# Modulation sums spread past the output projection, and a 32-byte tile in the last pool

## The chip, the cores and the metric

The kernel runs on one core of a Trainium2 chip. The metric is device time of one execution in microseconds (us), the median of several runs. Before the change it is 2329.75 us, the median of three (2326.13 to 2329.98).

## The reference, cut to what matters

One encoder layer for a sequence of 512 rows of width 2048, in fp32:

```
mod = silu(c) @ w_ada + b_ada                     # six vectors of 2048: sh1, sc1, gt1, sh2, sc2, gt2
h   = rms_norm(x, g_norm1) * (1 + sc1) + sh1
proj = h @ w_in                                   # q, k, v of 8 differential heads; latents of 8 MLA heads
a_out = subln(softmax(q1 k1 + bias) - lam * softmax(q2 k2 + bias)) @ v
b_out = latent attention with rotary tails
x   = x + gt1 * (concat(a_out, b_out) @ w_out)    # the output projection, residual x1
h2  = rms_norm(x, g_norm2) * (1 + sc2) + sh2      # needs all of x1's row, sh2 and sc2
x   = x + gt2 * ((silu(h2 @ w_gate) * (h2 @ w_up)) @ w_down)
```

## The kernel before

**Three matmuls for one.** Every fp32 product is computed from split operands: hi is the value rounded to TensorE's fp32r format, lo the remainder, and `mm3` (L240 to L243) issues hi*hi, lo*hi and hi*lo. Weights are split on the way: a chunk of 128x1024 is loaded into one of 3 `raw` buffers (L73), ScalarE casts hi (L89), and VectorE or GpSimd subtracts to get lo (L97). Which of the two does it stands in the plan: "dve", "pool", or "alt" for taking turns. There are two buffers for lo in these stages, so a split waits until TensorE is done with the chunk two before, and a load until the chunk three before is split.

**Stages.** Input projection and both attentions run to about 780 us. Then the output projection goes over four column blocks of 512 (L1072): blocks 0, 2 and 3 have 96 matmuls left, block 1 has 192, in chunks of 24; behind each block stand its residual (L1053 multiplies by `gt1`, L1054 adds to `x1`), a store of `x1` to DRAM (`x1d`, read back at the very end), and the squares' sums on ScalarE (L1102). The transposes of a block's `x1` (L1060) stand 36 matmuls into the next block. After block 3 come its transposes, the reciprocal root `rstd2` (a reduction on VectorE, two steps on GpSimd, L260 and L261) and its broadcast by matmul (`ps_r`). Then two gate/up column blocks in plain form (`gate_up`, 384 matmuls each), whose operand `h2` is built on the way by `second_norm` (L1134 to L1136) and `combine`; then the other gate/up blocks in a Strassen-like form to about 1818 us, and the down projection (`ps_d`, 2112 matmuls), which reads activations back from DRAM into `ax` tiles.

**The second modulation.** `mod2` (L1069) is a generator for columns 1024 to 2047 of sc2 and sh2. For each of two groups of 4 column chunks it loads 32 pieces of `w_ada` (256 KB each, L301) into `x1` slots, of which there are 24 (X_SLOTS), shared with `x1`, its transposes and the sums; VectorE multiplies each by a column of silu(c) and adds it to `adaacc` (L305, L308: the sums, 64 in all); then `ada_columns` turns the two sums of a group into columns by eight matmuls against a vector of ones (`ps_ada`, L327; each is recorded twice). That makes 78 steps, and `MOD_PACE` says how many are taken at each of the 8 or 16 yields (12 matmuls) of a block; `second_norm` takes what is missing for its group.

**Order.** TensorE's order is the order of the calls. The other engines' queues, and the loads on SP's queue, are put in order by the language's scheduler from its own estimates, so a number in `MOD_PACE` moves instructions on all of them. Each engine runs its queue in order: an instruction that waits holds all behind it.

**Places in SBUF.** The last pool, `fd` (L1351), is filled from the right-hand end: `sums`, `gt2`, then the `ax` tiles and `x1r`. In the built program the `ax` tiles begin at byte 126,944 of each partition, 32 beyond a multiple of 64, in steps of 2,048; the split weights of the down stage begin at 44,480 and on in steps of 4,096, multiples of 64. `ax` is the stationary operand of the down matmuls, the weights the moving one. In the output projection and gate/up both operands lie 32 beyond a multiple of 64; in the scores of the differential heads both lie at one.

Of the kernel before, what the change touches and what calls it, by code (L numbers as in the profile page):

```python
# [10 lines left out]
F32 = mybir.dt.float32  # L11
F32R = mybir.dt.float32r
AF = mybir.ActivationFunctionType
ALU = mybir.AluOpType
AX = mybir.AxisListType
# [3 lines left out]
P = 128  # L19
D = 2048  # L20
S = 512
NT = S // P
# [114 lines left out]
def weight_plan(a):  # L137
    w_in = a["w_in"][0]
    qkv = w_in[:, 0:3 * H * P].rearrange("(k p) (s n) -> p k s n", p=P, s=3)
    plan = []  # L140

    def rows(w, r0, nk, c0, n):
        return w[r0:r0 + nk * P, c0:c0 + n].rearrange("(k p) n -> p k n", p=P)

    def add_in(h, j):
        plan.append((("in", h, j), [2, 384], qkv[:, 2 * j:2 * j + 2, :, h * P:(h + 1) * P],
                     "dve" if h < FIRST else "pool"))

    for k0, nk in BLOCKS:
        for h in range(FIRST):  # L150
            for j in range(k0 // 2, (k0 + nk) // 2):
                add_in(h, j)
    for h in range(FIRST, H):
        for j in range(KC // 2):
            add_in(h, j)
    c0 = 3 * H * P
    for i in range(2):
        for j in range(KC // 4):
            plan.append((("cq", i, j), [4, 256], rows(w_in, j * 512, 4, c0 + i * 256, 256), "pool"))
    for j in range(KC // 2):  # L160
        plan.append((("ckv", j), [2, 320], rows(w_in, j * 256, 2, c0 + QL, 320), "pool"))

    def add_out(b, j0, j1):
        for j in range(j0, j1):
            plan.append((("out", b, j), [2, 512], rows(a["w_out"][0], j * 256, 2, b * 512, 512), OUT_SPLIT))

    for pr in range(4):
        for j in range(2):
            plan.append((("qb", pr, j), [2, 384], rows(a["w_q_b"][0], j * 256, 2, pr * 384, 384), "pool"))
        plan.append((("kvb", pr), [2, 512], rows(a["w_kv_b"][0], 0, 2, pr * 512, 512), "pool"))  # L170
        if pr == 1:
            add_out(2, 0, 4)
        elif pr == 3:
            add_out(3, 0, 4)
    add_out(0, 0, 8)
    add_out(1, 0, 8)
    add_out(2, 4, 8)
    add_out(3, 4, 8)

    for j in range(STRAIGHT):  # L180
        for k4 in range(4):
            for n in ("gate", "up"):
                plan.append(((n, j, k4), [4, 256], rows(a["w_" + n][0], k4 * 512, 4, j * 256, 256), "alt"))
    return plan


# [12 lines left out]
def hybrid_layer(ctx, tc, a, out):  # L199
    nc = tc.nc  # L200
    act, dve, pool, pe, sp = nc.scalar, nc.vector, nc.gpsimd, nc.tensor, nc.sync
# [56 lines left out]
    def rsqrt(dst, src, scale, eps=EPS):  # L258
        n = src.shape[-1]
        pool.tensor_scalar(out=dst, in0=src, scalar1=scale, scalar2=eps, op0=ALU.mult, op1=ALU.add)  # L260
        pool.tensor_tensor(out=dst, in0=dst, in1=mhalf[:, :n], op=ALU.pow)  # L261
# [26 lines left out]
    x1d = dram.tile([S, D], F32, name="x1d")  # L288
# [99 lines left out]
    for kind in LOADS:  # L388
# [4 lines left out]
        else:  # L393
            t, b = divmod(i, 4)
# [677 lines left out]
    for b in range(4):  # L1072
        tag = next_tag()
        spare[0] = "tmp" if tag == "acc" else "acc"
        if b == 0:
            assert tag == "acc"
            pss = half[0]
        else:
            pss = [bank(tag, "ps_o") for _ in range(NT)]
        j0 = 0 if b == 1 else 4  # L1080
        for i, _ in enumerate(project(pss, mixT, 512, [("out", b, j) for j in range(j0, 8)], 2 * j0, KC - 2 * j0,
                                      first=(b > 0))):
            if b == 0 and i == 1:
                sp.dma_start(out=gt1, in_=rowd[0:1, :].broadcast_to([P, D]))
            if b == 0 and i < 8:
                for t in range(2 * (i % 2), 2 * (i % 2) + 2):
                    sp.dma_start(out=x1[t][i // 2], in_=x[t * P:(t + 1) * P, i // 2 * 512:(i // 2 + 1) * 512])
            if b == 1 and i % 2 and i < 16:
                b2, t = 2 + i // 8, i % 8 // 2
                pool.tensor_tensor(out=half[b2][t], in0=half[b2][t], in1=gt1[:, b2 * 512:(b2 + 1) * 512], op=ALU.mult)  # L1090
                pool.tensor_tensor(out=x1[t][b2], in0=x1[t][b2], in1=half[b2][t], op=ALU.add)
            due += MOD_PACE[b]
            while due >= 1:
                due -= 1
                next(mod2, None)
            if i == 2 and b > 0:
                transposes(b - 1, spare[0])
        for t in range(NT):
            residual(pss, b, t, gt1, pool if t in OUT_POOL and b < 3 else dve)
            sp.dma_start(out=x1d[t * P:(t + 1) * P, b * 512:(b + 1) * 512], in_=x1[t][b])  # L1100
            sq = tmp("sq")
            act.activation(sq, x1[t][b], AF.Square, accum_out=ssq2[:, t, b:b + 1])  # L1102
            if b == 3:
                dve.tensor_reduce(out=rstd2[:, t:t + 1], in_=ssq2[:, t, :], axis=AX.X, op=ALU.add)
                rsqrt(rstd2[:, t:t + 1], rstd2[:, t:t + 1], 1.0 / D)
    while G2_done[0] < 3:
        next(mod2)
    transposes(3, spare[0])
# [19 lines left out]

    def second_norm(k0):
        while G2_done[0] <= k0 // 4:  # L1130
            next(mod2)
        for kc in range(k0, k0 + 4):
            xt = x1T[kc]
            dve.scalar_tensor_tensor(out=xt, in0=xt, scalar=G2[:, kc:kc + 1], in1=rB, op0=ALU.mult, op1=ALU.mult)  # L1134
            act.activation(h2(kc, 0), half_rows(xt), AF.Identity, bias=SH2[:, kc:kc + 1])
            dve.scalar_tensor_tensor(out=h2(kc, 1), in0=half_rows(xt), scalar=SH2[:, kc:kc + 1], in1=f(h2(kc, 0)),  # L1136
                                     op0=ALU.add, op1=ALU.subtract)
# [22 lines left out]
    def gate_up(j, between):  # L1160
        tag = next_tag()
        spare[0] = "tmp" if tag == "acc" else "acc"
        pg = [bank(tag, "ps_g") for _ in range(2)]
        pu = [bank(tag, "ps_u") for _ in range(2)]
        for k4 in range(4):
            for n, pp in (("gate", pg), ("up", pu)):
                wh, wl = W.get((n, j, k4))
                if n == "gate" and j == 0 and k4 < 3:
                    second_norm(4 * k4 + 4)
                for i in range(4):  # L1170
                    kc = k4 * 4 + i
                    for m in range(2):
                        mm3(pp[m], wh[:, i, tsl(m)], wl[:, i, tsl(m)], h2(kc, 0), h2(kc, 1), kc == 0, kc == KC - 1)
                    if G2_done[0] < 4:
                        next(mod2, None)
                next(between, None)
        sg = wp.tile([P, 1024], F32, tag="raw", bufs=3, name="sg").rearrange("p (m s) -> p m s", m=2)
        for m in range(2):
            act.activation(sg[:, m], pg[m], AF.Silu)
            dve.tensor_tensor(out=sg[:, m], in0=sg[:, m], in1=pu[m], op=ALU.mult)  # L1180
        sp.dma_start(out=actd[2 * j:2 * j + 2].rearrange("f p s -> p f s"), in_=sg)
# [102 lines left out]
    def load_acts(i):  # L1284
        j0 = sum(PARTS[:i])
        r = []
        for kt in range(2 * j0, 2 * (j0 + PARTS[i])):
            if i == 0:
                both = wp.tile([P, 1024], F32R, tag=("raw", "lo")[kt % 2], bufs=(3, 2)[kt % 2], name="act0")
                ah, al = both[:, :512], both[:, 512:]  # L1290
                if kt % 4 == 0:
                    avs = fw[0][1].tile([P, 8, 256], F32, tag="wr", bufs=3, name="av0").rearrange(
                        "p (k a) b -> p k (a b)", k=4)
                av = avs[:, kt % 4]
            else:
                ah, al = [fd[1].tile([P, S], F32R, tag="ax", bufs=32, name="ax") for _ in range(2)]
                av = fd[1].tile([P, S], F32, tag="x1r", bufs=4, name="av")
            sp.dma_start(out=av, in_=actd[kt])
            act.copy(out=ah, in_=av)
            minus(al, av, f(ah))  # L1300
            r.append((ah, al))
        acts[i] = r
# [48 lines left out]
    fd = open_pool("fd", "right")  # L1351
    sums = [[fd[1].tile([P, 512], F32, tag="sums", bufs=16, name="sums") for _ in range(4)] for _ in range(NT)]
    gt2 = fd[1].tile([P, D], F32, name="gt2")

    def gate2():
        def raws():
# [13 lines left out]

    side = gate2()
    load_acts(1)
    W = Wd
    n_parts = len(PARTS)
    j = 0
# [48 lines left out]
DIFF_SIDE = (1, 2, 1, 2, 1, 2, 1, 1)  # L1424
MLA_SIDE = (1, 2)
MOD_EARLY = 8
MOD_PACE = (0.3, 2.8, 3.4, 3.2)
MLA_STEPS = "s0 F t0 e F1 t1 s1 v0 F t2 F1 v1 t3 s2 F v2 F1 o0 v3 F o2 o3 s3 o1 F1"
MLA_FILL = (16.0, 15.7, 16.0, 0.2, 14.1, 19.0, 3.3, 12.8)

# [37 lines left out]
```

## Time and profile before

| | us |
|---|---|
| median of three runs | 2329.75 |
| the profiled execution | 2330.51 |
| its span (first to last instruction) | 2328.1 |
| TensorE busy | 2208.3 |
| VectorE, ScalarE, GpSimd busy | 1634.0, 944.7, 442.9 |
| mean granted clock | 0.984 |

Around the span lie 2.4 us. Busy time is a sum over stages with different limits, so it tells which engine is nearly full and not where time can be had; for that the waits of that engine, stage by stage, are read. TensorE's clock has two levels, 1.2 and 2.4 GHz; the granted clock is a mean share of the higher. Matmuls are pipelined, so the time that one takes by itself (0.39 us for 512 columns) is longer than the step from one start to the next, and it is the step that counts.

### The profile page before, as it was taken

How to read it: one execution, taken by the hardware profiler on the slowest of the kernel's cores; microseconds unless marked ns; L12 is line 12 of the kernel's file. 1: busy time of each engine (PE TensorE's matmuls, PEld its weight loads, DVE VectorE, ACT ScalarE, POOL GpSimd, SP SyncE). 2: the span in 40 equal slices, each digit the busy share in tenths (PEclk: the TensorE clock that was granted, in tenths of full speed). 3: DMA queues.
4: the chain of work that ended last, by engine and by line, in shares of the span. 5: the costliest groups of instructions: out<-in, count | busy, mean ns of one | idle time of the engine just before them, and what ended most of it. 6: DMA issues, size and time to landing. Idle time of an engine off the chain costs nothing.

```text
span 2328.1 us, 35444 instructions
## 1 busy us (share of the span) xinstructions
PE 2208.3 (95%) x13878; PEld 2011.6 (86%) x13878; DVE 1634.0 (70%) x2365; ACT 944.7 (41%) x1569; POOL 442.9 (19%) x492
## 2 busy tenths in 40 slices
PE   2799999999989997999999999999999999999999
PEld 2799989998877785789999999999999877888887
DVE  6987777868898575847777777777777577232543
ACT  4423545566555222434444444444444522121211
POOL 0002433445553622210000000000000221222221
PEclk9899999999999998999999999999999999999999
DMA  9965345422442585243333333333333775232532
GB/s 298 323 216 147 103 138 156 139 88 85 152 157 79 191 286 182 78 131 118 127 115 121 111 126 119 123 112 121 118 127 118 247 263 195 99 128 91 170 129 99
DMA packets 270569, 344.98 MB, mean 148 GB/s; under 512 B 14749, under 2 KB 170886, under 8 KB 270274
## 3 DMA queue, kind: packets, MB, share of 16 engines
q1 hardware_dynamic: 269912, 342.37, 44.9%
q8 instruction: 108, 1.77, 0.3%
q10 hardware_dynamic: 490, 0.36, 0.1%
q14 instruction: 59, 0.48, 0.1%
HBM read 322.71 MB, written 19.96 MB: 147 GB/s over the span
## 4 chain that ended last, share of the span: by engine, by line
PE 57%; DVE 6%; DMA 4%; issue 1%; ACT 1%; SPq 0%; POOL 0%; DVEq 0%; ACTq 0%
PE ps_d L243 6%; PE ps_d L241 6%; PE ps_d L242 6%; PE ps_X L1235 5%; PE ps_X L1236 5%; PE ps_X L1237 5%; PE ps_W L1235 3%; PE ps_W L1236 3%; PE ps_W L1237 3%; DVE adaacc L308 2%; DMA araw<-in_w_ada_dram 2%; PE ps_Y L1235 2%; PE ps_Z L1235 2%; PE ps_Y L1236 2%; PE ps_Z L1236 2%; PE ps_Z L1237 2%
## 5 line engine op out<-in xcount | busy, mean ns | idle before, releaser
L97 POOL TENSOR_TENSOR lo<-raw,hi 128x1024 fp32r<-128x1024 f32 (+1 forms) x75 | 183.6, 2448 | 1403.3 <-ACT hi L89 1384.5
L89 ACT CAST hi<-raw 128x1024 fp32r<-128x1024 f32 (+2 forms) x228 | 221.0, 970 | 508.4 <-PE ps_d L242 286.6
L97 DVE TENSOR_TENSOR lo<-raw,hi 128x768 fp32r<-128x768 f32 (+2 forms) x153 | 168.5, 1101 | 188.5 <-ACT hi L89 184.2
L1235 PE MATMUL ps_X<-comb,wh 128*128 128x256 f32 x960 | 269.7, 281 | 0.0
L1218 ACT CAST wh<-wr 128x1024 fp32r<-128x1024 f32 x160 | 168.6, 1054 | 247.5 <-PE ps_X L1236 69.1
L1236 PE MATMUL ps_X<-comb,wh 128*128 128x256 f32 x960 | 268.8, 280 | 0.0
L1237 PE MATMUL ps_X<-comb,wl 128*128 128x256 f32 x960 | 266.9, 278 | 0.0
L243 PE MATMUL ps_d<-lo,ax 128*128 128x512 f32 x640 | 254.7, 398 | 6.5 <-DVE lo L97 6.5
L241 PE MATMUL ps_d<-hi,ax 128*128 128x512 f32 x640 | 254.3, 397 | 0.0
L242 PE MATMUL ps_d<-hi,ax 128*128 128x512 f32 x640 | 254.1, 397 | 0.0
L1201 DVE TENSOR_TENSOR wl<-wr,wh 128x1024 fp32r<-128x1024 f32 x160 | 195.6, 1222 | 80.2 <-ACT wh L1218 80.0
L241 PE MATMUL ps_in<-hi,hh 128*128 128x384 f32 (+2 forms) x704 | 236.5, 336 | 6.1 <-ACT hi L89 2.7
L243 PE MATMUL ps_in<-lo,hh 128*128 128x384 f32 (+2 forms) x704 | 230.9, 328 | 8.5 <-DVE lo L97 8.5
L242 PE MATMUL ps_in<-hi,hl 128*128 128x384 f32 (+2 forms) x704 | 230.2, 327 | 0.6 <-DVE hl L382 0.6
L1218 ACT CAST wh<-wt 128x1024 fp32r<-128x1024 f32 x120 | 126.2, 1051 | 197.5 <-PE ps_X L1236 120.9
L1201 DVE TENSOR_TENSOR wl<-wt,wh 128x1024 fp32r<-128x1024 f32 x120 | 146.8, 1223 | 81.1 <-ACT wh L1218 81.1
L1236 PEld LDWEIGHTS ps_X<-comb,wh 128*128 128x128 f32 x960 | 180.5, 188 | 0.0
L1237 PEld LDWEIGHTS ps_X<-comb,wl 128*128 128x128 f32 x960 | 180.5, 188 | 0.0
L1235 PE MATMUL ps_W<-comb,wh 128*128 128x256 f32 x640 | 180.0, 281 | 0.4 <-DVE cu L1246 0.4
L1235 PEld LDWEIGHTS ps_X<-comb,wh 128*128 128x128 f32 x960 | 180.2, 188 | 0.0
L1236 PE MATMUL ps_W<-comb,wh 128*128 128x256 f32 x640 | 179.2, 280 | 0.0
L1237 PE MATMUL ps_W<-comb,wl 128*128 128x256 f32 x640 | 177.9, 278 | 0.0
(319 smaller groups left out, 5533.4 us busy)
## 6 DMA issues: line engine op xcount, KB each, us to landing
araw<-in_w_ada_dram SPq DMA_DIRECT2D x96, 512.0 KB
raw<-in_w_down_dram SPq DMA_DIRECT2D x88, 512.0 KB
wr<-in_w_gate_dram SPq DMA_DIRECT2D x40, 1024.0 KB
wr<-in_w_up_dram SPq DMA_DIRECT2D x40, 1024.0 KB
ada<-in_w_ada_dram SPq DMA_DIRECT2D x128, 256.0 KB
raw<-in_w_in_dram SPq DMA_DIRECT2D x128, 192.0 KB
raw<-in_w_out_dram SPq DMA_DIRECT2D x32, 512.0 KB
x<-in_w_ada_dram SPq DMA_DIRECT2D x64, 256.0 KB
```

Of the source, the lines that this page charges most:

```text
L89: nc.scalar.copy(out=hi[:, :n], in_=raw[:, :n])
L97: e.tensor_tensor(out=lo[:, :n], in0=raw[:, :n], in1=hi[:, :n].bitcast(F32), op=ALU.subtract)
L241: pe.matmul(o, ah, bh, start=start, stop=False)
L242: pe.matmul(o, al, bh, start=False, stop=False)
L243: pe.matmul(o, ah, bl, start=False, stop=stop)
L308: dve.scalar_tensor_tensor(out=acc[:, :width], in0=raw[:, i, :width], scalar=c_col[:, q:q + 1], in1=acc[:, :width], op0=ALU.mult, op1=ALU.add)
L1201: dve.tensor_tensor(out=out, in0=x, in1=y, op=ALU.subtract)
L1218: act.copy(out=hi, in_=src)
L1235: pe.matmul(ps[bk], wh[:, k], c[:, 0], start=first and k == 0, stop=False, skip_group_check=True)
L1236: pe.matmul(ps[bk], wh[:, k], c[:, 1], start=False, stop=False, skip_group_check=True)
L1237: pe.matmul(ps[bk], wl[:, k], c[:, 0], start=False, stop=k == 7, skip_group_check=True)
```

## The change

Six edits:

1. the lo splits of the up chunks of the two plain gate/up blocks go from GpSimd to VectorE (the plan's "alt" becomes "dve"; the gate chunks were on VectorE);
2. the 16 stores of `x1d` are issued on ScalarE's queue after each block, and not on SP's queue after each row tile;
3. `rstd2` is reduced and rooted once for all four row tiles;
4. `MOD_PACE` for blocks 1 to 3 falls from 2.8, 3.4, 3.2 to 2.0, 2.5, 2.5: 74.4 steps inside the projection where 78 are needed, so that the second `ps_ada` group falls to `second_norm`;
5. `gate_up` no longer takes steps of `mod2` between its matmuls, and `second_norm` may run to the generator's end;
6. a tile of 32 bytes per partition is put into `fd` behind `gt2`, so that `ax` and `x1r` lie 32 bytes lower (`ax` at 126,912 and on, multiples of 64). 1920 of the 2112 down matmuls read `ax`; the first 192 read activations kept elsewhere, 32 beyond a multiple of 64, before and after.

```diff
@@ weight_plan
-                plan.append(((n, j, k4), [4, 256], rows(a["w_" + n][0], k4 * 512, 4, j * 256, 256), "alt"))
+                plan.append(((n, j, k4), [4, 256], rows(a["w_" + n][0], k4 * 512, 4, j * 256, 256), "dve"))
@@ after each column block
             residual(pss, b, t, gt1, pool if t in OUT_POOL and b < 3 else dve)
-            sp.dma_start(out=x1d[t * P:(t + 1) * P, b * 512:(b + 1) * 512], in_=x1[t][b])
             sq = tmp("sq")
             act.activation(sq, x1[t][b], AF.Square, accum_out=ssq2[:, t, b:b + 1])
-            if b == 3:
-                dve.tensor_reduce(out=rstd2[:, t:t + 1], in_=ssq2[:, t, :], axis=AX.X, op=ALU.add)
-                rsqrt(rstd2[:, t:t + 1], rstd2[:, t:t + 1], 1.0 / D)
+        for t in range(NT):
+            act.dma_start(out=x1d[t * P:(t + 1) * P, b * 512:(b + 1) * 512], in_=x1[t][b])
+    dve.tensor_reduce(out=rstd2, in_=ssq2, axis=AX.X, op=ALU.add)
+    rsqrt(rstd2, rstd2, 1.0 / D)
@@ second_norm
-            next(mod2)
+            next(mod2, None)
@@ gate_up
-                    if G2_done[0] < 4:
-                        next(mod2, None)
@@ the last pool
     load_acts(1)
+    pads.append(fd[1].tile([P, 8], F32, name="pad"))
-MOD_PACE = (0.3, 2.8, 3.4, 3.2)
+MOD_PACE = (0.3, 2.0, 2.5, 2.5)
```

**TensorE, 24 matmuls into block 3, before.** `ps_o` are the projection's sums, `ps_ada` the second modulation's columns.

```order
L242 MATMUL ps_o<-hi,ml 128x512
L243 MATMUL ps_o<-lo,mh 128x512
L327 MATMUL ps_ada<-ones,adaacc 128x1 [waits DVE_49]
L327 MATMUL ps_ada<-ones,adaacc 128x1 x3
L327 MATMUL ps_ada<-ones,adaacc 128x1 [waits DVE_49]
L327 MATMUL ps_ada<-ones,adaacc 128x1 x3
L241 MATMUL ps_o<-hi,mh 128x512 [waits Activation_49]
L242 MATMUL ps_o<-hi,ml 128x512
```

**TensorE, in the first gate/up block, 96 matmuls in, after.** `ps_u` and `ps_g` are up and gate.

```order
L242 MATMUL ps_u<-comb,lo 128x512
L243 MATMUL ps_u<-comb,hi 128x512
L327 MATMUL ps_ada<-ones,adaacc 128x1 x8
L241 MATMUL ps_g<-comb,hi 128x512 [waits Activation_49]
L242 MATMUL ps_g<-comb,lo 128x512 [waits DVE_49]
```

The eight `ps_ada` matmuls have left block 3, whose 96 matmuls now follow each other, and stand 96 matmuls into gate/up. (The first group has moved too, from block 1 to 24 matmuls into block 2.)

**VectorE at the residual of block 3, before.** L308 is a sum, L97 a lo split, L1053 and L1054 the residual of the first row tile.

```order
L308 SCALAR_TENSOR_TENSOR adaacc<-x_9705,c_col,adaacc 128x512 [waits DMAHW1_49,DVE_49]
L308 SCALAR_TENSOR_TENSOR adaacc<-x_9708,c_col,adaacc 128x512 [waits DMAHW3_49,DVE_49]
L308 SCALAR_TENSOR_TENSOR adaacc<-x_9723,c_col,adaacc 128x512 [waits DMAHW5_49,DVE_49]
L328 TENSOR_TENSOR G_95<-ps_ada,small 128x4 [waits PE_49]
L330 TENSOR_TENSOR SH_96<-ps_ada,small 128x4
L329 TENSOR_TENSOR G_95<-G_95,small 128x4 [waits DVE_49]
L1157 TENSOR_TENSOR shs<-SH_96 128x8 [waits DVE_49]
L97 TENSOR_TENSOR lo<-raw,hi 128x1024 [waits DMAHW0_49,PE_49,Activation_49]
L1053 TENSOR_TENSOR tm<-ps_o,gt_8892 128x512 [waits PE_49]
L1054 TENSOR_TENSOR x_8879<-x_8879,tm 128x512 [waits DVE_49,Pool_49]
```

**The same place after.**

```order
L308 SCALAR_TENSOR_TENSOR adaacc<-x_9857,c_col,adaacc 128x512 [waits DMAHW5_49,DVE_49]
L308 SCALAR_TENSOR_TENSOR adaacc<-x_9860,c_col,adaacc 128x512 [waits DMAHW6_49,DVE_49]
L97 TENSOR_TENSOR lo<-raw,hi 128x1024 [waits DMAHW7_49,PE_49,Activation_49]
L308 SCALAR_TENSOR_TENSOR adaacc<-x_9863,c_col,adaacc 128x512 [waits DMAHW7_49,DVE_49]
L1053 TENSOR_TENSOR tm<-ps_o,gt_8892 128x512 [waits PE_49]
L308 SCALAR_TENSOR_TENSOR adaacc<-x_9884,c_col,adaacc 128x512 [waits DMAHW0_49,DVE_49]
L1054 TENSOR_TENSOR x_8879<-x_8879,tm 128x512 [waits DVE_49,Pool_49]
L308 SCALAR_TENSOR_TENSOR adaacc<-x_9887,c_col,adaacc 128x512 [waits DMAHW1_49,DVE_49]
L1053 TENSOR_TENSOR tm<-ps_o,gt_8892 128x512 [waits PE_49]
L1054 TENSOR_TENSOR x_8883<-x_8883,tm 128x512 [waits DVE_49,Pool_49]
```

The last sum stood well ahead of the residual, with the `ps_ada` columns taken from it (L328 to L330) in between; now 62 sums stand ahead of the residual's first step, the split of the first gate chunk (L97) among the last of them, and the last two sums between its steps.

**SP's queue at the last loads of the modulation, before.** Each L301 is a piece of `w_ada` for one sum, L73 a weight chunk, L1100 a store of `x1d`.

```order
L301 DMA x_9681<-in_w_ada_dram 128x512 [waits DMAHW0_49,DVE_49]
L301 DMA x_9702<-in_w_ada_dram 128x512 [waits DMAHW1_49,DVE_49]
L301 DMA x_9705<-in_w_ada_dram 128x512 [waits DMAHW2_49,DVE_49]
L1100 DMA x1d<-x_8878 128x512
L301 DMA x_9708<-in_w_ada_dram 128x512 [waits DMAHW3_49,DVE_49]
L1100 DMA x1d<-x_8882 128x512 [waits DMAHW4_49]
L301 DMA x_9723<-in_w_ada_dram 128x512 [waits DMAHW5_49,DVE_49]
L1100 DMA x1d<-x_8886 128x512 [waits DMAHW6_49]
L1100 DMA x1d<-x_8890 128x512 [waits DMAHW7_49,DVE_49]
L73 DMA raw<-in_w_gate_dram 128x4x256 [waits DMAHW0_49,Pool_49]
L73 DMA raw<-in_w_up_dram 128x4x256 [waits DMAHW1_49,DVE_49]
```

**The same place after.**

```order
L73 DMA raw<-in_w_out_dram 128x2x512 [waits DMAHW5_49,Activation_49]
L73 DMA raw<-in_w_gate_dram 128x4x256 [waits DMAHW7_49,Pool_49]
L301 DMA x_9739<-in_w_ada_dram 128x512 [waits DMAHW1_49,DVE_49]
L301 DMA x_9742<-in_w_ada_dram 128x512 [waits DMAHW6_49,DMAHW2_49,DVE_49]
L301 DMA x_9745<-in_w_ada_dram 128x512 [waits DMAHW3_49,DVE_49]
L301 DMA x_9766<-in_w_ada_dram 128x512 [waits DMAHW5_49,DMAHW0_49,DVE_49]
L301 DMA x_9769<-in_w_ada_dram 128x512 [waits DMAHW6_49,DVE_49]
L73 DMA raw<-in_w_up_dram 128x4x256 [waits DMAHW7_49,DVE_49]
L301 DMA x_9812<-in_w_ada_dram 128x512 [waits DMAHW0_49,PE_49]
L301 DMA x_9815<-in_w_ada_dram 128x512 [waits DMAHW2_49,DMAHW1_49,DVE_49]
L301 DMA x_9818<-in_w_ada_dram 128x512 [waits DMAHW4_49,PE_49,Activation_49]
```

The loads of the first gate and up chunk have moved ahead of the last 15 and the last 10 loads of `w_ada`, and the stores are gone from this queue. The up chunk's load waits for a split on VectorE.

## Rows read from the trace of the kernel before

**Rows 1.** The page: busy us (share of the span) and instructions of each engine.

```profile
PE 2208.3 (95%) x13878; PEld 2011.6 (86%) x13878; DVE 1634.0 (70%) x2365; ACT 944.7 (41%) x1569; POOL 442.9 (19%) x492
```

**Rows 2.** TensorE's waits, 780 to 1040 us: total, times, longest.

```profile
PE ps_ada L327 <- DVE adaacc L308: 11.0, 1, 11.0
...
PE ps_xT L1060 <- DVE x L1054: 3.4, 2, 2.9
```

**Rows 3.** TensorE's timeline, block 3: start, us, tile, count, [idle before <- releaser].

```profile
887.73 0.95 PE L327 MATMUL ps_ada<-ones,adaacc 128*128 128x1 f32 x8
899.63 1.87 PE L327 MATMUL ps_ada<-ones,adaacc 128*128 128x1 f32 x8 [10.95 <-DVE adaacc L308]
...
901.93 0.63 PE L242 MATMUL ps_o<-hi,ml 128*128 128x512 f32 x1
...
905.34 0.63 PE L241 MATMUL ps_o<-hi,mh 128*128 128x512 f32 x1
...
910.84 0.39 PE L241 MATMUL ps_o<-hi,mh 128*128 128x512 f32 x1
...
921.50 0.39 PE L243 MATMUL ps_o<-lo,mh 128*128 128x512 f32 x1
```

**Rows 4.** Windows: busy us (instructions) of each engine, granted clock, DMA share, GB/s.

```profile
860.00:890.00 30.00, 27.80 (x133) 22.56 (x131) 23.40 (x27) 9.55 (x18) 7.72 (x3) 1.00 0.84 277
890.00:920.00 30.00, 20.37 (x89) 17.21 (x90) 12.41 (x22) 6.55 (x11) 2.39 (x1) 0.77 0.36 116
950.00:980.00 30.00, 28.57 (x123) 22.41 (x121) 29.96 (x56) 16.12 (x25) 6.83 (x2) 1.00 0.21 68
1840.00:1880.00 40.00, 40.00 (x173) 32.22 (x172) 25.21 (x31) 18.20 (x28) 7.72 (x4) 1.00 0.81 276
```

**Rows 5.** VectorE's timeline: a sum and block 2's last residual step; two late steps.

```profile
880.67 0.75 DVE L308 SCALAR_TENSOR_TENSOR adaacc<-x,c_col,adaacc 128x512 f32<-128x512 f32 x1 [2.65 <-DMA x<-in_w_ada_dram]
...
894.08 0.67 DVE L1054 TENSOR_TENSOR x<-x,tm 128x512 f32<-128x512 f32 x1
...
935.61 2.07 DVE L1136 SCALAR_TENSOR_TENSOR comb<-x1T,SH,comb 128x512 fp32r<-128x512 f32 x3
...
946.59 3.72 DVE L1136 SCALAR_TENSOR_TENSOR comb<-x1T,SH,comb 128x512 fp32r<-128x512 f32 x3 [0.26 <-ACT comb L1135]
```

**Rows 6.** Timelines of ScalarE, VectorE and GpSimd: squares, residual of block 3, GpSimd's splits.

```profile
892.32 0.63 ACT L1102 ACTIVATE sq<-x 128x512 f32<-128x512 f32 x1 [3.96 <-DVE x L1054]
...
917.38 1.22 DVE L97 TENSOR_TENSOR lo<-raw,hi 128x1024 fp32r<-128x1024 f32 x1 [15.41 <-ACT hi L89]
...
924.12 2.62 DVE L1054 TENSOR_TENSOR x<-x,tm 128x512 f32<-128x512 f32 x1
...
923.86 2.34 POOL L97 TENSOR_TENSOR lo<-raw,hi 128x1024 fp32r<-128x1024 f32 x1
...
946.01 2.42 POOL L97 TENSOR_TENSOR lo<-raw,hi 128x1024 fp32r<-128x1024 f32 x1 [17.34 <-ACT hi L89]
```

**Rows 7.** Waits of SP's own queue, 770 to 960 us: total, times, longest.

```profile
SPq L1100 <- DVE x L1054: 25.1, 12, 4.8
```

**Rows 8.** Down matmuls: TensorE's waits from 1820; the tile's operations; its timeline.

```profile
PE ps_d L243 <- DVE lo L97: 6.5, 4, 2.7
...
L241 PE MATMUL ps_d<-hi,ax x640: 392/396/628, 1862.9 to 2322.5; 128*128 128x512 f32 x160
...
L241 PE MATMUL ps_d<-hi,act x64: 395/396/397, 1818.1 to 1862.2; 128*128 128x512 f32 x64
...
1999.61 0.40 PE L243 MATMUL ps_d<-lo,ax 128*128 128x512 f32 x1
...
2002.41 0.40 PE L243 MATMUL ps_d<-lo,ax 128*128 128x512 f32 x1
```

**Rows 9.** TensorE's timeline: scores of a differential head.

```profile
252.75 0.39 PE L679 MATMUL ps_s<-k,q 128*128 128x512 f32 x1
...
253.43 0.39 PE L680 MATMUL ps_s<-klo,q 128*128 128x512 f32 x1
```

More of the change, by code (lines that the diff above doesn't have):

```diff
@@ L1353, in hybrid_layer @@
     gt2 = fd[1].tile([P, D], F32, name="gt2")
+    pads = []
     def gate2():
```

## The prediction

> **What bounds the kernel now.** The first view is the page's table of busy times: TensorE works 2208.3 of 2328.1 us, so two things can shorten the run: its idle time, 120 us, and the pace of its matmuls [rows 1]. Nothing is edited ahead of the output projection. The second view is therefore TensorE's waits from 780 to 1040 us, the projection and the first two gate/up blocks. One entry towers over the rest: the transposing matmuls `ps_ada` wait 11.0 us, once, for the last accumulated `adaacc` sum [rows 2]. The third view, its timeline, shows the place, 24 matmuls into the last column block: the half of the second `ps_ada` group on the scale sum starts at 887.73, the half on the shift sum at 899.63 after 10.95 us of idleness [rows 3]. The windows beside it show why: up to 890 us the DMA engines are busy 0.84 of the time at 277 GB/s, since 64 loads of modulation weights, 256 KB each, are to come in inside the projection, and in the following window TensorE has 20.37 of 30 us at a granted clock of 0.77 [rows 4]. From about 1820 us on TensorE is full (40.00 of 40) and waits only 6.5 us in all [rows 4, 8]; there only pace counts.
>
> **The removed stall.** In the changed order the second `ps_ada` group stands in the gate/up block, and the matmuls of the last block run on. That removes 10.95 us. The stall also lowers the clock: eight matmul steps behind it take (905.34 - 901.93) / 8 = 0.426 us each, against (921.50 - 910.84) / 47 = 0.2268 later: the 1.2 GHz level and the 2.4 one [rows 3]. Ten matmuls at 0.2 us extra are 2.0 us, and the second half of `ps_ada` took 1.87 where the first took 0.95 [rows 3], 0.9 more. Together 13.9 us. The ordinary 1.9 us of the group are only moved.
>
> **What is late next.** The slower pace leaves 22 of the 64 sums behind the first residual step of block 2, where before it was 12; 20 of them stand ahead of the residual of the last block, and two between its steps. TensorE would reach the end of the last block at 921.50 + 0.23 - 13.9 - 1.9 = about 906 us on the old trace's clock [rows 3]; its first row tile, done 9 matmuls earlier, waits for VectorE from 904. Does VectorE get there? On SP the load of the first up chunk now stands ahead of the last ten sums' loads; it needs the raw buffer that VectorE's split of chunk (3,6) frees, and that split waits for the first 24 matmuls of the block, done at 887.73 [rows 3]. VectorE is then in block 2's residual, whose last step ends at 894.75 in the old trace [rows 5]; with fewer sums ahead of it I take 891, and SP free at 892 after the split. Ten loads of 256 KB and one of 512 KB are 3.1 MB, at 277 GB/s [rows 4] 11.4 us: the 62nd sum at about 904. So by this estimate from rows it just makes it. Two further terms: in the residual itself two sums (0.75 each) and the split of the up chunk (1.22) now stand in the line, +2.7 us, against which the 2.62 us step of the residual that ran beside GpSimd's split goes back to some 0.67, -1.9 us [rows 5, 6]; and the transposes of block 2, hidden behind the stall before, now come at about 891, 36 matmuls into the last block, while their last residual step ends about then or two us later: +1 us. I add 2 us for loads that arrive late. Projection: -13.9 + 2.7 - 1.9 + 1 + 2 = -10.1 us, with ends at -14 (all on time) and 0 (the stall comes back whole at the residual).
>
> **The stores of `x1d`.** SP waited 25.1 us at these 12 stores for residuals that weren't ready [rows 7]; the loads behind them were held. On ScalarE's queue they come after each block's squares. There they hold nothing that TensorE needs: the next hi casts need a raw chunk and a released buffer, and what the stores wait for in the changed order are DMA lanes whose loads VectorE has used by then. Each costs ScalarE an issue; SP's and ScalarE's issues aren't among busy rows, so I bound each from below by nothing and from above by the square that it follows, 0.63 [rows 6]: 0 to 10 us in all, over 130 us in which ScalarE is busy about a third [rows 4]. I take no cost, and no gain either, since the loads it frees meet DMA engines at 0.84; ends +2 and -3.
>
> **The reductions of `rstd2`.** Four reductions and eight GpSimd steps become one and two. The last one decides before and after; the others ran beside TensorE's transposes. Zero, within 0.5 us.
>
> **The gate/up splits.** Eight splits of 128x1024 go from GpSimd to VectorE, 8 x 1.22 = +9.8 us of VectorE work. But GpSimd's splits stretch VectorE: three `L1136` steps took 3.72 us beside one and 2.07 without, 1.65 more; the residual step lost 1.95 [rows 5, 6]. Eight times 1.65 to 1.95 is 13 to 16 us if each hits; in the second block VectorE has room and may stand idle under one, so I count five: -9 us. VectorE is full from 950 to 980 (29.96 of 30) where TensorE has 28.57 [rows 4], so a net change there passes on. Zero, with ends -3 and +5. The second `ps_ada` group adds three small steps, and its sums were finished long before.
>
> **The pad.** The tile of 32 bytes lets all `ax` tiles start 32 bytes lower: at a multiple of 64 instead of 32 beyond one, as the split weights of this stage do; weights are the moving operand, `ax` the stationary one. Rows that compare such pairs: down matmuls (unequal) start every (2002.41 - 1999.61) / 12 = 0.2333 us; those of the first part, whose operands are unequal too, every (1862.2 - 1818.1) / 189 = 0.2333 (64 of each of the three operations, so 63 x 3 steps) [rows 8]. Matmuls of the same shape in the projection, where both lie at 32, start every 0.2268 [rows 3], and scores of the differential heads, both at 0, (253.43 - 252.75) / 3 = 0.2267 [rows 9]. So it goes with equal residues, not with a residue of its own. If the 1920 matmuls on `ax` (3 x 640 [rows 8]) take that pace, the gain is 1920 x 0.00667 = 12.8 us; the 192 of the first part keep theirs. A faster TensorE meets its weights earlier: the 6.5 us of waits may grow, DMA is up to 0.81 busy there [rows 4]. I take -12. The other end is 0; a loss has no row for it, and I keep +3 for waits that a changed meeting of loads could bring.
>
> A rule speaks against this. The Trainium skill ("SBUF — State Buffer", Who interferes with whom) gives TensorE two independent read ports, one for the moving operand and one for the weights load, and says that it never waits on anyone; by that, where two operands lie can't change a pace, and this term is 0. The rows above show two paces at one shape without an engine beside that explains it, so I go by the rows; the rule's outcome is the first rival.
>
> **Sum.** -10.1 + 0 + 0 + 0 - 12 = -22.1 us, on the profiled execution's 2330.5 (2328.1 in the span and 2.4 around it): 2308.4. The median of the runs shown is 0.8 lower, so I predict 2307.5 us.
>
> **The rivals.**
> 1. The pad gives nothing: the two paces come from something else that differs between stages, such as the buffers' owner or what VectorE reads. For it: each stage has one pair of residues, so stage and pair can't be told apart in steady streams; against: the short runs of equal pairs in the attention. Then 2330 - 10 = 2319.5. Chance 0.22.
> 2. The stall only moves: the sums are bound by the DMA engines (0.84 busy [rows 4]), and the 3.1 MB behind the up chunk come when TensorE is already done; the residual of the last block then waits as long as `ps_ada` did. The pad alone stays: 2329.75 - 12 = 2317.5. Chance 0.12.
> 3. Slower. The last ten loads go one after another: each takes a slot of the 24 that an earlier sum frees, and VectorE stands behind its in-order split of the first gate chunk, which waits until 72 of the block's 96 matmuls are done. If only one load is under way at a time, each costs its landing and a sum. The nearest row is a sum that waited 2.65 us for its load and took 0.75 [rows 5]: ten such are 34 us, from 892 to 926. The residual then starts 22 us late, with 2 us of half clock behind it as after the old stall: -13.9 + 24 = +10, and with a pad that does nothing 2340. It decides from about 14 us of lateness on; with the pad's 12 it needs 26. Against it: the order lets at least five loads be out together. Chance 0.05, the worse half of gate/up included.
> 4. Neither mechanism takes hold, or they cancel: 2327 to 2333. Chance 0.07.
>
> **How the numbers follow.** My forecast has 0.54: both terms, 2307.5 with its own range 2303 to 2313. The range for all is 2301 to 2322: below it lie the cases in which the projection gains all 14 and gate/up 3 more, above it the last two rivals. A measurement of this kernel can tell 0.2%, 4.7 us, from no change. Faster than that are my case and the first two rivals, 0.88; within it the fourth, 0.07; slower the third, 0.05.
>
> **What would show it.** After the change, TensorE's waits from 780 to 1040 have no `ps_ada` entry above 1 us, and the granted clock of the last block stays at full. The longest wait there should be `ps_xT` on the residual, at most 5 us; 10 or more means the second rival. The step from one down matmul to the next reads 0.2267 behind the first part and 0.2333 in it; 0.2333 in both means the first. GpSimd's splits vanish between 940 and 1020, and VectorE's steps of 3.72 with them. What would make the prediction wrong is a new wait of TensorE for a lo split in block 3, as VectorE's split of chunk (3,6) now stands behind 49 sums and the residual of block 2.

## The result and the profile after

The changed kernel takes 2303.02 us (median of four, 2301.07 to 2303.95) where the one before took 2327.94 beside it; the ratio is 0.9882, 95% interval 0.9868 to 0.9897. The forecast was 2307.5, some 5 us too slow. The profiled execution has a span of 2299.3 us.

TensorE's timeline cuts both kernels at the same matmuls. The second columns are another profiled execution of the same kernel; all in us:

| stage | before | again | after | again |
|---|---|---|---|---|
| start to last attention score | 766.3 | 772.2 | 769.8 | 771.4 |
| to the first gate matmul (projection) | 165.0 | 165.4 | 151.6 | 152.6 |
| plain gate/up | 94.9 | 94.2 | 91.8 | 90.9 |
| Strassen-like units | 791.9 | 793.4 | 784.6 | 785.8 |
| down, first 192 matmuls | 44.8 | 44.8 | 44.8 | 44.8 |
| down, the 1920 on `ax` | 460.1 | 458.5 | 451.7 | 446.9 |
| span | 2328.1 | 2333.5 | 2299.3 | 2297.4 |

A span ends 5.1 us behind the start of the last down matmul, which the lines leave out. The first line belongs to the executions, not to the change: nothing was edited there, and two executions of before alone give 766.3 and 772.2. The others are read one by one.

TensorE's waits of after, 770 to 1040 us (total, times, longest):

```profile
PE ps_xT L1060 <- DVE x L1054: 5.3, 4, 2.9
PE ps_o L243 <- POOL lo L97: 3.4, 2, 3.1
PE ps_g L241 <- ACT comb L1135: 1.6, 1, 1.6
PE ps_r L1111 <- POOL rstd L261: 1.3, 1, 1.3
```

The 11.0 us of `ps_ada` [rows 2] are gone, and the transposes that wait for a residual stand first. Where, VectorE's timeline shows, and behind it TensorE's, at the end of block 3:

```profile
905.83 1.22 DVE L97 TENSOR_TENSOR lo<-raw,hi 128x1024 fp32r<-128x1024 f32 x1
906.97 0.74 DVE L308 SCALAR_TENSOR_TENSOR adaacc<-x,c_col,adaacc 128x512 f32<-128x512 f32 x1
907.63 0.68 DVE L1053 TENSOR_TENSOR tm<-ps_o,gt 128x512 f32<-128x512 f32 x1
...
914.60 0.69 DVE L1054 TENSOR_TENSOR x<-x,tm 128x512 f32<-128x512 f32 x1
```

```profile
906.47 0.39 PE L243 MATMUL ps_o<-lo,mh 128*128 128x512 f32 x1
909.72 0.93 PE L1060 MATMUL ps_xT<-ident,x 128*128 128x128 f32 x4 [2.86 <-DVE x L1054]
...
921.42 0.79 PE L241 MATMUL ps_g<-comb,hi 128*128 128x512 f32 x1 [1.59 <-ACT comb L1135]
```

The last projection matmul starts at 906.47, but the residual's first step only at 907.63, behind the sums and the split of the first gate chunk. From the last projection matmul to the first gate one it is 14.95 us, against 9.73 before. Windows of after (columns as in [rows 4]):

```profile
880.00:900.00 20.00, 18.88 (x91) 15.28 (x90) 18.82 (x23) 7.76 (x15) 5.69 (x2) 1.00 0.90 302
900.00:910.00 10.00, 7.14 (x33) 5.66 (x32) 9.56 (x14) 1.45 (x2) 0.00 (x0) 1.00 0.88 289
...
950.00:980.00 30.00, 30.00 (x134) 24.86 (x133) 29.60 (x55) 17.43 (x30) 0.00 (x0) 1.00 0.36 113
```

From 880 on TensorE works 18.88 of 20 us at a granted clock of 1.00, where from 890 to 920 before it had 20.37 of 30 at 0.77 [rows 4]; in the window from 900 it stops with the end of the block. The DMA engines are busy 0.9 up to that end. Gate/up is full at 950 to 980 with VectorE at 29.60 of 30. The down matmuls, by the tile's operations and two of its rows:

```profile
L241 PE MATMUL ps_d<-hi,act x64: 393/396/396, 1797.8 to 1841.9; 128*128 128x512 f32 x64
...
1999.80 0.39 PE L243 MATMUL ps_d<-lo,ax 128*128 128x512 f32 x1
...
2002.52 0.39 PE L243 MATMUL ps_d<-lo,ax 128*128 128x512 f32 x1
```

Twelve steps on `ax` take 2.72 us, 0.2267 each, where they took 2.80 [rows 8]; on the first part's activations, not moved, (1841.9 - 1797.8) / 189 = 0.2333 as before.

### The profile page after: what moved, and what is told of

Read it like the earlier page. It is cut to its first block, busy times and chain, and to the rows that moved or that the text cites. A ratio compares the mean times of both kernels' runs of the same rounds, so it can differ in the third digit from the quotient of the medians.

```text
span 2299.3 us, 35409 instructions
## 1 busy us (share of the span) xinstructions
PE 2190.4 (95%) x13878; PEld 2005.4 (87%) x13878; DVE 1633.7 (71%) x2370; ACT 944.5 (41%) x1569; POOL 419.8 (18%) x478
## 3 DMA queue, kind: packets, MB, share of 16 engines
q1 hardware_dynamic: 267608, 338.18, 44.8%
## 4 chain that ended last, share of the span: by engine, by line
PE 60%; DVE 7%; DMA 5%; issue 2%; POOL 1%; ACT 0%; SPq 0%; DVEq 0%; ACTq 0%; POOLq 0%
PE ps_d L243 6%; PE ps_d L241 6%; PE ps_d L242 6%; PE ps_X L1233 5%; PE ps_X L1234 5%; PE ps_X L1235 5%; PE ps_W L1233 3%; PE ps_W L1234 3%; PE ps_W L1235 3%; DVE adaacc L308 2%; DMA x<-in_w_ada_dram 2%; PE ps_Y L1233 2%; PE ps_Z L1233 2%; PE ps_Z L1234 2%; PE ps_Y L1234 2%
## 5 line engine op out<-in xcount | busy, mean ns | idle before, releaser
L97 POOL TENSOR_TENSOR lo<-raw,hi 128x1024 fp32r<-128x1024 f32 (+1 forms) x67 | 161.6, 2412 | 1387.5 <-DMA raw<-in_w_down_dram 878.4
L97 DVE TENSOR_TENSOR lo<-raw,hi 128x1024 fp32r<-128x1024 f32 (+2 forms) x161 | 178.4, 1108 | 170.9 <-ACT hi L89 166.8
L241 PE MATMUL ps_d<-hi,ax 128*128 128x512 f32 x640 | 250.9, 392 | 0.0
L242 PE MATMUL ps_d<-hi,ax 128*128 128x512 f32 x640 | 250.6, 392 | 0.0
```

Of the source, the lines that this page charges most:

```text
L97: e.tensor_tensor(out=lo[:, :n], in0=raw[:, :n], in1=hi[:, :n].bitcast(F32), op=ALU.subtract)
L241: pe.matmul(o, ah, bh, start=start, stop=False)
L242: pe.matmul(o, al, bh, start=False, stop=False)
```

## The experiments

Ratios are to the kernel before, run on the same chip, with 95% intervals where there were several runs; the rest is each profiled execution, in us.

| | ratio | projection | gate/up | units | down on `ax` |
|---|---|---|---|---|---|
| the tile alone | 0.9963 (0.9946 to 0.998) | 168.0 | 94.9 | 788.2 | 448.6 |
| edits 4 and 5 | 0.9937 (0.9914 to 0.996) | 153.9 | 94.5 | 785.0 | 459.6 |
| edits 1 to 3 | 0.9943 (0.9922 to 0.9964) | 160.0 | 90.3 | 787.7 | 457.1 |
| after, other PSUM banks | 0.9873 (0.9849 to 0.9898) | 152.8 | 92.1 | 789.2 | 447.4 |
| after, weights moved, not `ax` | 0.9955 (0.9937 to 0.9973) | 153.6 | 92.0 | 808.2 | 449.5 |
| 64-byte tile | one run | 165.2 | 94.3 | 790.9 | 459.9 |
| after again | 0.9873 (0.9836 to 0.9909) | 152.6 | 90.9 | 785.8 | 446.9 |
| edit 1 alone | one run | 164.2 | 91.0 | 787.4 | 460.4 |
| edit 2 alone | one run | 160.3 | 95.8 | 791.6 | 460.0 |
| after, 5 sums later | 0.986 (0.983 to 0.9889) | 149.8 | 92.2 | 785.8 | 447.0 |
| after, 10 sums later | 0.9889 (0.9861 to 0.9918) | 148.5 | 99.1 | 785.8 | 448.4 |

**The tile alone.**

```diff
     load_acts(1)
+    pads.append(fd[1].tile([P, 8], F32, name="pad"))
```

> The kernel before with the 32-byte tile alone. Theory A (equal residues of the two operands' addresses set the pace): the down matmuls on ax step at 0.2267 us instead of 0.2333, the stage behind its first part takes 451 to 452 us as in the changed kernel instead of 460, the Strassen-like units keep 791.9 us, the median falls by 8 to 12 us (ratio 0.995 to 0.9965). Theory B (the pace came with the earlier edits, the tile does nothing): 460 us there, ratio 1.000. If the units too fall to 784.6 us, the tile acts on them by something other than the addresses of their operands, which it does not move.

The stage on `ax` falls to 448.6: theory A, the tile acts by itself. The units' 788.2 lie between the two values of the theory (their two paces, below). The projection's 168.0 is 3 us above before's; the stretch from block 0's transposes to block 1's took 53.4 where the two executions of before had 49.1 and 50.4, so a single profile of that stretch carries some 3 us.

**The tile at 64 bytes.**

```diff
+    pads.append(fd[1].tile([P, 16], F32, name="pad"))
```

> The kernel before with a tile of 64 bytes in the place of the 32: ax moves by 64 bytes and keeps its residue. Theory residues: 0.2333 us a step and 457 to 460 us behind the first part, as before. Theory any shift or the tile's presence: 0.2267 and about 449.

TensorE's timeline, down matmuls of this kernel:

```profile
2099.80 0.40 PE L243 MATMUL ps_d<-lo,ax 128*128 128x512 f32 x1
...
2102.60 0.40 PE L243 MATMUL ps_d<-lo,ax 128*128 128x512 f32 x1
```

Twelve steps in 2.80 us, 0.2333: a shift that keeps the residue does nothing.

**Equal residues the other way round.** The tile in `fd` is left out, and the weights' pool begins with one instead.

```diff
         fw.append(open_pool("fw"))
+        fw.append(fw[0][1].tile([P, 8], F32, name="pad"))
...
-    pads.append(fd[1].tile([P, 8], F32, name="pad"))
```

> The changed kernel without its tile in the last pool, but with a 32-byte tile at the start of the weights' pool: split weights and ax both lie 32 beyond a multiple of 64, and so do the first part's activations and both operands of the units. Theory equal residues: all 2112 down matmuls step at 0.2267 us, the first part takes 43.5 us instead of 44.8, the rest 447 to 452. Theory ax at a multiple of 64 (the stationary operand's own residue): 0.2333, 44.8 and 457 to 460. For the units: if equal residues count at 256 columns as well, they leave the spread of 784.6 to 791.9 us seen so far; otherwise they stay in it.

The tile's operations, its timeline, and a window within the units:

```profile
L241 PE MATMUL ps_d<-hi,act x64: 389/389/396, 1823.9 to 1866.8; 128*128 128x512 f32 x64
...
2099.83 0.39 PE L242 MATMUL ps_d<-hi,ax 128*128 128x512 f32 x1
...
2102.55 0.39 PE L242 MATMUL ps_d<-hi,ax 128*128 128x512 f32 x1
...
1200.00:1240.00 40.00, 40.00 (x336) 40.00 (x335) 29.94 (x32) 17.28 (x21) 0.00 (x0) 1.00 0.36 119
```

With both operands 32 beyond a multiple of 64 the step is 2.72 / 12 = 0.2267 too, and the first part, whose operands have become equal as well, steps at 42.9 / 189 = 0.2270 instead of 0.2333. So it is the equality, as far as residues of 0 and 32 go. The units, 256 columns wide, answer the other way: with equal residues 808.2 us, longer than any other execution, 336 recorded matmuls in 40 us instead of 342 to 346. That costs more than the down stage gains, so this kernel, with edits 1 to 5 in it, is no better than the tile alone.

**The pace of MOD_PACE alone.** Edits 4 and 5:

```diff
-MOD_PACE = (0.3, 2.8, 3.4, 3.2)
+MOD_PACE = (0.3, 2.0, 2.5, 2.5)
...
-                    if G2_done[0] < 4:
-                        next(mod2, None)
```

> The kernel before with MOD_PACE, second_norm and gate_up as changed (edits 4 and 5), without the tile, the dve splits, the moved stores and the single reduction. Theory A (the projection's gain is the second ps_ada group's leaving block 3): the projection from the last attention score to the first gate matmul falls from 165 us to 150 to 157; down stage unchanged at 460. For the units two theories: their pace goes with the PSUM banks that ps_ada's place hands them, which are those of the changed kernel here: 784.6 us; or it goes with something else (addresses, other edits): 791.9 us. Ratio 0.992 with the units' gain, 0.9955 without.

The projection falls by 11.1 us, to 153.9: the stall's removal is these two edits'. The units took 785.0, which fits the first of their two theories; the run with other banks, below, takes that up.

**Edits 1 to 3 alone.**

> The kernel before with edits 1 to 3 alone: up splits on VectorE, x1d stores on ScalarE's queue, one reduction for rstd2. My theory: gate/up 95 us to 92 to 95, projection within 3 us of 165, units 791.9, down 460: ratio 0.997 to 1.001. Rival: the stores' move alone frees the loads of the modulation and removes most of the 11 us stall, the projection falls by 8 us or more: ratio 0.996 or below.

The theory missed: gate/up 90.3, the projection 160.0, the ratio 0.9943. The rival was nearer, with 5 us off the projection, half of the stall. Which of the edits, the next two tell, each by a single run.

**Edit 1 alone.** Only the plan's "alt" became "dve".

> The kernel before with the up chunks' splits on VectorE alone (edit 1). Theory: the 4.6 us that edits 1 to 3 together took off gate/up (94.9 to 90.3) are this edit's, since GpSimd's splits no longer hold VectorE: 90 to 91.5; the projection keeps 165 within 1.5 us. Rival: they come from the queues (stores off SP, earlier weights): gate/up stays at 94 to 95.

Gate/up takes 91.0, the projection 164.2: theory. TensorE's waits for splits in that stage, before:

```profile
PE ps_g L242 <- DVE lo L97: 1.5, 1, 1.5
PE ps_u L242 <- POOL lo L97: 0.7, 2, 0.5
```

With 0.5 for a cast and 0.5 for `comb`, TensorE waited 3.2 us there behind the first gate matmul; with edit 1 alone it is 1.4, and in after nothing. Windows of the kernel with edit 1 alone:

```profile
940.00:970.00 30.00, 30.00 (x134) 24.86 (x133) 27.76 (x47) 16.01 (x23) 0.00 (x0) 1.00 0.28 88
970.00:1000.00 30.00, 30.00 (x134) 24.86 (x133) 20.99 (x39) 14.40 (x24) 0.00 (x0) 1.00 0.66 209
```

TensorE is full in both, and VectorE has 2.2 us to spare in the first although it has more splits to do.

**Edit 2 alone.** The stores go to ScalarE's queue after each block.

> The kernel before with the stores of x1d on ScalarE's queue alone (edit 2). Theory: the 4.9 us that edits 1 to 3 took off the projection (block 2 to 3: 41.0 to 35.5) are this edit's, since loads no longer stand behind stores that wait for the residual: 35 to 37 there, gate/up unchanged at 94 to 95. Rival: the projection gains nothing here and the gain was the single reduction's or the order's.

Gate/up stays (95.8), and from block 1's transposes to block 2's it is 33.1 instead of 41.0, less than the 35 to 37 expected. TensorE's wait and one of SP's, same kernel:

```profile
PE ps_ada L327 <- DVE adaacc L308: 5.1, 2, 4.4
...
SPq L301 <- DMA x<-in_w_ada_dram: 7.5, 11, 1.9
```

The longest wait of `ps_ada` falls from 11.0 to 4.4: theory. SP's 25.1 us at the stores [rows 7] had held back the loads on which that stall waited: at block 2's first residual step 7 of the 64 sums are left, as with edits 1 to 3, where before 12 were. The run's time, 2330.26 us, lies within that of before beside it (2325.33 to 2335.80), so this rests on the stage and on the run of edits 1 to 3.

**Other PSUM banks for the units.**

```diff
+    for tg, k in (("acc", 2), ("tmp", 2)):
+        for _ in range(k):
+            dve.memset(bank(tg, "ps_turn")[:, 0:1], 0.0)
```

> The changed kernel with four small VectorE fills of spare PSUM banks ahead of the units, so that their sums lie in other banks (X in 4, 3, 5, 0 instead of 6, 0, 4, 2). Theory banks: the units' pace moves away from 784.6 us, to 791.9 or between. Theory not banks: 784.6 us within 1, ratio to the kernel before as the changed kernel's, 0.988 to 0.990.

789.2: between the two, which the theory of banks allows; but within the execution the pace changed once with the banks as they were, so banks alone don't set it (below).

**Both kernels once more.**

> The changed kernel once more, for what one execution differs from the next. If the units' 784.6 us belong to the change, they come out within 1 us of that, as does the stage ahead of the last score (769.8). If it is the execution, they lie anywhere from 784 to 792, and the first stage from 766 to 772.

> The kernel before once more. If the units' 791.9 us belong to it, within 1 us of that; if to the execution, from 784 to 792. Projection 163 to 166, gate/up 94 to 96, down behind the first part 457 to 460.

The units came within 1.5 us of their first values in each, a little outside the 1 us expected; the first stage of before moved by 6 us. By that the units' gain looks like the change's; the window counts say what it is. Three windows of the kernel with the 64-byte tile, one execution:

```profile
1300.00:1340.00 40.00, 40.00 (x342) 40.00 (x341) 30.30 (x31) 17.75 (x22) 0.00 (x0) 1.00 0.38 123
...
1500.00:1540.00 40.00, 40.00 (x346) 40.00 (x345) 30.98 (x32) 17.72 (x22) 0.00 (x0) 1.00 0.36 119
1700.00:1740.00 40.00, 40.00 (x342) 40.00 (x342) 30.63 (x32) 17.36 (x22) 0.00 (x0) 1.00 0.37 124
```

The same matmuls on the same addresses run at one of two paces, 117.78 ns a step or 116.67 by the starts, and pass from one to the other and back. Over 6720 steps that is 7.5 us. Each passage lies at a short break of TensorE, a step of 0.15 to 1.25 us. Such a break in the kernel with edit 2 alone, on VectorE's and on TensorE's timeline:

```profile
1377.56 1.23 DVE L1202 TENSOR_TENSOR wt<-wr,wt 128x1024 f32<-128x1024 f32 x1 [1.40 <-DMA wr<-in_w_gate_dram]
...
1379.84 0.41 DVE L1247 TENSOR_TENSOR cu<-cu,ps_W 128x256 f32<-128x256 f32 x1
...
1380.31 0.39 PE L1236 MATMUL ps_W<-comb,wh 128*128 128x256 f32 x1 [0.78 <-DVE cu L1247]
```

A weight load lands late, VectorE's `cu` stands behind it, and TensorE waits 0.78 us for a bank; ahead of this break the pace was the faster one, behind it the slower. After other breaks it stayed. Both executions of before had the slower one from the second or third unit on; after had the faster one throughout, in both.

**Fewer sums ahead of the last residual.** The last number of `MOD_PACE` 1.5 instead of 2.5; then 2.2 and 1.2 for the last two.

```diff
-MOD_PACE = (0.3, 2.0, 2.5, 2.5)
+MOD_PACE = (0.3, 2.0, 2.5, 1.5)
```

> The changed kernel with 1.5 in the place of the last 2.5 of MOD_PACE: 59 sums stand ahead of the residual of block 3 instead of 62 to 64, the last 5 go to the gate/up block. Theory: the residual's lateness (14.95 to 15.3 us from the last projection matmul to the first gate one, 9.7 before the change) is the sums' and their loads', at 0.9 of the DMA engines: it falls to 10 to 12 us, and gate/up takes at most 2 us more; ratio to the kernel before 0.985 to 0.988. Rival: the split of the first gate chunk in VectorE's queue holds the residual whatever the sums: 14 to 15 us stay, ratio 0.9875 to 0.989.

> As e9 with 2.2 and 1.2 for blocks 2 and 3: 54 sums ahead of the residual, 10 in gate/up. Theory: 9.7 to 11 us from the last projection matmul to the first gate one; the second ps_ada group 96 matmuls into gate/up then waits for its sums, 0 to 6 us, so gate/up takes 92 to 99 us and the sum is about e9's or worse. Rival as in e9: 14 to 15 us.

From the last projection matmul to the first gate one: 12.5 us, just outside the 10 to 12 expected, and 10.7, after 14.95. So the sums hold the residual, though with five fewer it is a part only: VectorE's first step still starts at 908.95, behind the gate chunk's split, with the matmuls at their end. With ten fewer the second `ps_ada` group waits, in that kernel's timeline:

```profile
948.32 1.86 PE L327 MATMUL ps_ada<-ones,adaacc 128*128 128x1 f32 x8 [5.31 <-DVE adaacc L308]
```

Gate/up takes 99.1 then. Five later sums are the best of these, 2299.29 us in the median of four, but the interval holds the changed kernel's ratio too: not told apart.

## Why the prediction was right or wrong

**What failed.** The forecast was too slow. Three of its steps failed: the zero for the gate/up splits, the worst mis-sized term (edit 1 alone gained 3.2 to 3.9 us); "no gain" for the stores, whose move alone took 5 us off the projection; and the units, for which the sum had no term at all.

**The removed stall: right.** From block 1's transposes to block 2's it is 41.04 us before and 24.23 after, 16.8 less, where 13.9 and the moved 1.9 were forecast. Edits 4 and 5 alone give the same 24.21. Ahead of that stretch the projection is another 2.7 us shorter (2.9 in the second pair, 2.2 with edits 4 and 5 alone), for which the forecast had no term and no run shows the cause. Of the second rival, a stall that only moves, some 6 us came true.

**What is late next: right in mechanism, too small.** Forecast +2.7 - 1.9 + 1 + 2 = 3.8 us; measured 5.2 at the end (14.95 against 9.73) and 1.0 from block 2's transposes to the last matmul (16.16 against 15.17), together 6.2. Of the 5.2 some 3.6 are the residual's and the rest the root's (below). The 62nd sum was put at about 904 and ended at 907.7: VectorE came to the gate chunk's split only at 905.83, after loads at 0.88 to 0.90 of the DMA engines. Another cause was left out of the sum: beside GpSimd's split in this block a sum is stretched too, as VectorE's and GpSimd's timelines of after show.

```profile
897.82 4.02 DVE L308 SCALAR_TENSOR_TENSOR adaacc<-x,c_col,adaacc 128x512 f32<-128x512 f32 x3 [0.40 <-DMA x<-in_w_ada_dram]
902.01 3.90 DVE L308 SCALAR_TENSOR_TENSOR adaacc<-x,c_col,adaacc 128x512 f32<-128x512 f32 x5 [0.18 <-DMA x<-in_w_ada_dram]
...
896.97 2.69 POOL L97 TENSOR_TENSOR lo<-raw,hi 128x1024 fp32r<-128x1024 f32 x1 [9.14 <-ACT hi L89]
```

Three sums take 4.02 us where five take 3.90 later, some 1.7 us more, and from 892 us to the split VectorE's waits for loads are 0.40 us at most, 1.3 together. Which of the two weighs more was not varied.

**The stores: wrong.** "No gain, since the loads it frees meet DMA engines at 0.84" failed: alone, the move takes 6.6 us off the longest wait and 5 off the projection. That a mean share of 0.84 left gaps in which held loads could run is argued and not shown. What the move is worth beside edits 4 and 5, with which the stall is gone anyway, was not run: the projection is 153.9 with those two alone, 151.6 and 152.6 with all.

**The splits: the mis-sized term.** Zero was forecast for them, and 1.9 us for the `ps_ada` group that moves in; the stage gained 3.2. Edit 1 alone gives 91.0 against 94.9 and 94.2, and ends below the lower bound of -3. Five stretched steps were set against eight splits so that they cancelled. What the sum left out is what late splits cost TensorE itself. Behind the first 8 us of the stage, steps longer than the pace of 0.2267 cost it 5.4 us in before and 4.8 in its second execution, 1.4 with edit 1 alone, and 1.8 in after, which is the `ps_ada` group that moved in. Of the 5.4, waits are 2.7 (1.5 for one of VectorE's splits, 0.7 for GpSimd's, which take 2.42 us against 1.22 [rows 6], 0.5 for a cast), and the rest is slower steps next to them.

**The reductions: a small loss where zero within 0.5 us was forecast.** The root of all four row tiles takes longer, and `ps_r` waits for it: 1.3 us in after, 1.3 to 1.8 in every kernel with edit 3, with edits 1 to 3 alone too, and not at all in those without it. "The last one decides before and after" was wrong: in before the first `ps_r` matmuls started 0.95 us ahead of the end of the last row tile's root, and now all of them wait for the one root.

**The pad: right in place and pace, a little too large.** 0.2267 behind the first part and 0.2333 in it, as forecast; the first rival is out. The stage gained 8.5 us in the profiled pair, 11.6 in the second one, and the tile alone 10 to 11.5, where -12 was forecast. The pace is worth its 12.8 in each; what the stage takes beyond 1919 steps at the pace is 12.4 and 10.8 us in before, 16.7 and 12.0 in after. Windows of after in that stage:

```profile
1883.00:1923.00 40.00, 32.81 (x132) 25.86 (x131) 32.27 (x36) 6.83 (x7) 7.71 (x4) 0.92 0.70 245
1923.00:1963.00 40.00, 40.00 (x169) 32.90 (x168) 21.05 (x25) 12.29 (x16) 7.20 (x3) 0.95 0.50 166
```

TensorE is idle for 7 of 40 us there, and the granted clock is at 0.92 and 0.95: breaks and their half-speed stretches take what is missing. The Trainium skill ("SBUF — State Buffer", Who interferes with whom) says that TensorE never waits on anyone. That section is on what one engine does to another, and reading it as a term of 0 went beyond it; here the pace changes with where TensorE's own two operands lie, so the measurement decides.

**The units: no term in the sum.** It was taken for granted that a stage whose instructions aren't edited keeps its time; 7.3 us of the profiled pair are the two paces. Whether the edits favour the faster one stays open. All seven executions with the old `MOD_PACE` have a slower stretch, and the five with the new one, its banks and unequal residues have none; but the kernel with other banks has one too, and what else differs between those groups (banks, the moments at which loads land) was not varied one by one.

**Sum.** By stages the forecast was -12.0 for the projection, +1.9 for gate/up, 0 for the units and -12 behind them, -22.1. The profiled pair gave -13.3, -3.2, -7.3 and -8.5, and +3.5 in the first stage: -28.8. Without the units' pace and the first stage, which no edit is shown to set, it is -25.0, and the gate/up splits are what was most mis-sized, 5.1 us.

## What to carry to other kernels

Where TensorE is full, compare the step between starts of equal matmuls across stages: a difference of 3% with no wait behind it pointed at the operands' addresses, and a few bytes in a pool put it right, but the better residue depends on the width, so each stage is tried by itself. A store that waits for a late result belongs on a queue with no loads behind it, even where the DMA engines look busy on average. When a stall is taken out of an in-order queue, count what still stands ahead of the next instruction that matters: five fewer sums there gave back another 2.4 us of the 5.2.

## What the runs showed of the hardware

- At 512 columns in this number format, the down matmuls step at 0.2267 us when the stationary and the moving operand start at equal residues modulo 64 bytes (0 and 0, or 32 and 32) and at 0.2333 when they are 32 apart. Other residues were not tried. At 256 columns, in the one kernel that has them, equal residues are the slower ones, 120.0 ns a step (808.2 us for the units) against 116.67 or 117.78.
- With unequal residues at 256 columns there are two paces, and a break of a fraction of a microsecond can change one to the other.
- The faster pace of equal residues comes only some steps behind a break. In gate/up before, at a granted clock of 1.00 [rows 4], ten steps soon after a wait take 2.32 us and the next ten 2.26:

```profile
961.87 0.50 PE L242 MATMUL ps_u<-comb,lo 128*128 128x512 f32 x1 [0.53 <-POOL lo L97]
...
962.45 0.40 PE L241 MATMUL ps_u<-comb,hi 128*128 128x512 f32 x1
...
964.77 0.39 PE L242 MATMUL ps_u<-comb,lo 128*128 128x512 f32 x1
...
967.03 0.39 PE L243 MATMUL ps_u<-comb,hi 128*128 128x512 f32 x1
```
